# A hybrid attention and state-space layer on one core: the mixer's splits, loads, result tiles and squares in another order

## The chip, the cores and the metric

The kernel runs on one core of a Trainium2 chip. The metric is the device time of one execution in microseconds (us): the median of a few runs. In the text PE is the matrix engine (PEld its weight load), DVE the vector engine, ACT the scalar engine, POOL GpSimd, and SP the engine whose queue issues nearly all the DMAs.

## The reference, cut to what matters

One layer, 1024 positions of width 1024, all in float32. The part around the change is the state-space mixer (its scan runs in the kernel in chunks of 256 positions) and the projection of the attention's result beside it:

```python
X = (xh * dt[..., None])                    # 32 heads of 64, 8 groups, state 128
a_cum = jnp.cumsum(dt * A)                  # per head, inside a chunk
Lmat = jnp.exp(jnp.where(causal, a_cum[:, None] - a_cum[None, :], -inf))
CB = C @ B.T                                # per group
y_diag = (CB * Lmat) @ X
states = B.T @ (decay * X);  h = h * exp(a_cum[-1]) + states
y_off = exp(a_cum) * (C @ h_before)
y = y_diag + y_off + d_skip * xh
y_b = rmsnorm(y * silu(z), ssd_norm) @ w_o_ssd
mix = (sigmoid(g_a) * (attention @ w_o_attn) + sigmoid(g_b) * y_b) @ w_out
```

Then a residual sum and a SwiGLU block follow, which the change does not touch.

## The kernel before, in words

Every large product is made of three float32r matmuls: an operand is rounded to `hi` (on ACT) and the rest is kept as `lo` (on DVE or POOL), and hi·hi, hi·lo and lo·hi are added up. A "split" is this pair of instructions.

The **mixer stage** is a loop of 32 steps, n = 4·group + chunk (loop at the end of the excerpt), and one more for the last results. A step holds:

- `ssd_in(c, g)` for step n: SP loads `ld` (B, C and x: L1163, L1164) and `al` (the cumulative decays, broadcast to all partitions: L1169). ACT makes four M and four al rows with Relu (L1174, L1175) and two exponentials (L1176). PE makes `pcb` (C·B, L1179); DVE masks it (`cbm`) and multiplies it into al and M (L1184). PE transposes x (`px`) and B (`pbn`), and DVE and POOL make `X` and `Xd`.
- `ssd_out(c, g)` for step n−1: SP loads `zc` (the gate silu(z): L1215) and, but for a group's first chunk, `yt` (the decays of the state's share: L1218, two DMAs). PE makes `pyd` (the diagonal part, from al, M and X: L1224, L1225), `pst` (the chunk's state) and `pyo` (the part of the state so far: L1234). DVE multiplies and adds (L1236, L1237) and adds d_skip·x (L1241, two halves); POOL multiplies by the gate (L1243); SP stores the result to `d_y` (L1244). ACT squares the result for the norm (L1247), DVE adds the squares up (L1254), and the state is scaled on POOL and added to on DVE (L1258, L1260).

`zc` and `yt` share one tile, the **home** of a result: for n divisible by 3 it is the one tile `vt`, else one of the eight 1024-column tiles of the arena `R`, which also holds `ld` and `al`.

Beside each step PE does three or four slices of a **filler** (`beside`), six 128x512 matmuls each: first gate projections (pw, L244), then the projection of the attention's result (`poa`, L244). For the latter, sixteen tiles of the attention's result are loaded (`at_load`) and split (`at_split`, L1299, L1303), in four bursts of four, between tiles of the filler. `poa_run` loads a gate tile `ya` (L1321), and stores the product (L1325). Before the projection's last three tiles, `y_load` loads twelve half rows of `d_y` that the first groups have finished, and splits them (L1267, L1277, L1278), all in one burst.

After the last step the filler's rest runs alone, and then the **output projection** `pos` (L1647, seven products for a Strassen-like scheme in `SEQ`), whose inputs are sums and splits of `d_y` rows (`tasks`), and whose weights are split on ACT and POOL, later on ACT and DVE (L158, L159). Two norms (`ry`: p, L271, POOL's power L273, prn L279) and the merges with the attention's branch (`merge_first`, `gates_of`) are placed between its products.

PE's order is the order of the code (`in_order`). The order on ACT, DVE, POOL and SP is set by a scheduler from the code's order, its own timeline, the tiles' reuse and added "behind" dependencies (`add_manual_dep` with NoSync: an order on one engine, no wait). All four work their instructions off strictly in that order.

Of the kernel before, what the change touches and what calls it, by code (L numbers as in the profile page):

```python
# [69 lines left out]
def build(tc, a, dbg=None, stop=99, slots=None):  # L70
# [1084 lines left out]
    exps = [None]  # L1155

    def ssd_in(c, g, out):

# [4 lines left out]
        SP.dma_start(bc, d_bc[g].rearrange("j p l -> p j l")[:, :, cl])  # L1163
        SP.dma_start(xs, d_xs[2 * g:2 * g + 2].rearrange("j p l -> p j l")[:, :, cl])  # L1164
# [4 lines left out]
        SP.dma_start(al, d_ac[c, hs][None].to_broadcast([P, 4, QC]))  # L1169
# [37 lines left out]
    def ssd_out(c, g, z):  # L1207
# [4 lines left out]
        zy = (vp.tile([P, NT, P], F32, name="vt", bufs=1).rearrange("p (j x) n -> p j (x n)", j=4) if (4 * g + c) % 3 == 0  # L1212
              else R("zy", (P, 4, 256)))
        zc, yt = zy[:, 0:2], zy[:, 2:4]
        SP.dma_start(zc, d_z[2 * g:2 * g + 2].rearrange("j p l -> p j l")[:, :, cl])  # L1215
        if c:
            for e in range(2):
                SP.dma_start(yt[64 * e:64 * e + 64],  # L1218
                             d_ea[c, hs].rearrange("(j e) l -> e j l", e=2)[e:e + 1].to_broadcast([64, 2, QC]))
# [11 lines left out]
        if c:  # L1231
            pyo = bank("pyo")
            for j in range(2):
                T.matmul(pyo[:, 256 * j:256 * j + 256], st[:, 128 * j:128 * j + 128], CT, start=True, stop=True)  # L1234
            ytf = yt.rearrange("p j l -> p (j l)")
            V.tensor_tensor(ytf, ytf, pyo, op=OP.mult)  # L1236
            V.tensor_tensor(ytf, ytf, pyd, op=OP.add)  # L1237
        else:
            S.activation(yt.rearrange("p j l -> p (j l)"), pyd, AF.Copy)
        for j in range(2):  # L1240
            V.scalar_tensor_tensor(yt[:, j, :], xs[:, j], dsk[:, 2 * g + j:2 * g + j + 1], yt[:, j, :],  # L1241
                                   op0=OP.mult, op1=OP.add)
        G.tensor_tensor(yt, yt, zc, op=OP.mult)  # L1243
        SP.dma_start(d_y[2 * g:2 * g + 2].rearrange("j p l -> p j l")[:, :, cl], yt)  # L1244
        yield
        sq = Q("ysqt", (P, 2, 256))
# [8 lines left out]
        if c == 0:  # L1255
            S.activation(st, pst[:, 0:256], AF.Copy)
        elif c < NCH - 1:
            G.tensor_tensor(st.rearrange("p (h n) -> p h n", h=4), st.rearrange("p (h n) -> p h n", h=4),  # L1258
                            cdec[:, c, hs, None].to_broadcast([P, 4, 64]), op=OP.mult)
            V.tensor_tensor(st, st, pst[:, 0:256], op=OP.add)  # L1260
        yield
# [20 lines left out]
    def y_load(ks, places):  # L1282
        for k in ks:
            y_parts(1 + k // SK, k % SK, y_raw(k, 0), places(k), col("ssd_norm", k))

    def beside():
# [9 lines left out]
        def at_split(b, ks, where, raws):  # L1296
            for t, k in zip(raws, ks):
                hi, lo = where("ath", dt=F32R), where("atl", dt=F32R)
                i = S.activation(hi, t, AF.Copy).ins  # L1299
                for j in (ahead[0], *exps[0]):  # L1300
                    tc.add_manual_dep(i, j, mybir.DependencyInfo(
                        mybir.DependencyClass.NoSync, mybir.DependencyReason.DATA), reason="behind")
                (G if k % 2 else V).tensor_tensor(lo, t, f(hi), op=OP.subtract)  # L1303
                AT[k][0][b], AT[k][1][b] = hi, lo

# [13 lines left out]
        def poa_run(t, b, w):  # L1319
            ya = EV("ya")  # L1320
            SP.dma_start(ya, d_sga[t][:, half(b)])  # L1321
# [3 lines left out]
            SP.dma_start(d_ya[t][:, half(b)], ya)  # L1325
# [11 lines left out]
        at_split(*ld)  # L1337
        ld = at_load(0, range(AT_IN_Q, KT), H_)
        yield from gate_run(7, 0, w[1])
        at_split(*ld)  # L1340
        ld = at_load(1, range(4), H_)
        yield from gate_run(6, 1, w[0])
        at_split(*ld)
        ld = at_load(1, range(4, KT), H_)
        yield from gate_run(7, 1, w[1])
        w = two_tiles(a["w_o_attn"], (0, 1))
        yield from poa_run(0, 0, w[0])
        at_split(*ld)
# [815 lines left out]
```

## Time and profile before

| what | us |
|---|---|
| three runs: median (lowest, highest) | 2359.7 (2351.64, 2362.59) |
| the profiled execution's own time | 2361.0 |
| its span, first to last instruction | 2359.2 |
| PE busy in the span | 2308.6 (98%) |
| DVE, ACT, POOL busy | 1658.4, 1220.9, 988.0 |
| the mixer's steps: first and last pcb matmul | 1121.4 to 1420.9 |
| last scan result on PE (pyo) and first output projection | about 1438 and 1454 |

PE is busy nearly all the time, so time is to be had only where it waits or runs slowly. In a row of a timeline stand start, duration, engine, line, operation, output and inputs, and in brackets the idle time before the instruction and what ended it. A row of waits has: who waited, for whom, total us, times, longest.

### The profile page before, as it was taken

To read this page: it belongs to the slowest core of one execution; us is meant where nothing else is said; L and a number is where in the kernel's file an instruction comes from. 1 tells how busy PE (TensorE), PEld (TensorE's weight loads), DVE (VectorE), ACT (ScalarE), POOL (GpSimd) and SP (SyncE) were. 2 spreads that over 40 slices of the span, in tenths; PEclk is the share of its full clock that TensorE was granted. 3 is DMA by queue.
4 is the path that set the end of the run, shared out by engine and by line. 5 is a ranking of instruction groups with operands and counts; after the bars stand their busy time and mean duration, and the time that the engine had idled before them with its cause. 6 is when DMAs were issued, how large, how long until landed. Compare 5 with 4: busy or idle time off the path is not lost.

```text
span 2359.2 us, 35056 instructions
## 1 busy us (share of the span) xinstructions
PE 2308.6 (98%) x11736; PEld 1889.5 (80%) x11736; DVE 1658.4 (70%) x3185; ACT 1220.9 (52%) x2362; POOL 988.0 (42%) x787
## 2 busy tenths in 40 slices
PE   8999999999999999999999989999999999999997
PEld 5878888888888888887887777878788888888887
DVE  5467887499676767776678769865868776646675
ACT  4346666467645555556667565444555222235542
POOL 1435552522245656554445443000113445554556
PEclk8999999999999999999999999999999999999999
DMA  7137542622233433344679888864483444428664
GB/s 271 63 122 246 191 175 94 192 94 94 103 110 118 140 128 128 126 139 154 215 238 291 250 272 277 278 202 143 144 277 138 151 149 154 158 96 285 209 189 168
DMA packets 251716, 411.27 MB, mean 174 GB/s; under 512 B 25568, under 2 KB 93328, under 8 KB 251536
## 3 DMA queue, kind: packets, MB, share of 16 engines
q1 hardware_dynamic: 238288, 387.48, 49.2%
q10 hardware_dynamic: 13248, 21.56, 3.0%
q8 instruction: 92, 1.51, 0.3%
q14 instruction: 88, 0.72, 0.1%
HBM read 304.84 MB, written 107.24 MB: 175 GB/s over the span
## 4 chain that ended last, share of the span: by engine, by line
PE 74%; DVE 11%; DMA 7%; ACT 3%; issue 2%; POOL 1%; SPq 1%; DVEq 0%; ACTq 0%; POOLq 0%
PE p L1723 18%; PE pw L234 14%; PE pfo L1988 8%; PE pw L244 7%; PE plg L847 4%; PE pos L1647 3%; PE pot L1435 3%; PE prel L648 3%; PE pt L880 3%; PE po L896 3%; DVE junk L702 2%; PE puq L234 2%; DMA yl<-d_y 2%; PE poa L244 2%; DMA d_y<-zy 1%
## 5 line engine op out<-in xcount | busy, mean ns | idle before, releaser
L159 POOL TENSOR_TENSOR wlo<-wraw,whi 128x512 fp32r<-128x512 f32 x152 | 210.4, 1385 | 334.0 <-ACT whi L158 307.7
L1723 PE MATMUL p<-xh,wr 128*128 128x512 f32 x880 | 271.8, 389 | 0.0
L158 ACT ACTIVATE whi<-wraw 128x512 fp32r<-128x512 f32 x238 | 149.1, 627 | 214.0 <-issue 57.4
L1723 PEld LDWEIGHTS p<-xh,wr 128*128 128x128 f32 x880 | 165.2, 188 | 34.3
L1717 POOL TENSOR_TENSOR wr<-a,wr 128x512 fp32r<-128x512 f32 x82 | 115.2, 1413 | 134.0 <-ACT wr L1716 97.8
L1723 PE MATMUL p<-xl,wr 128*128 128x512 f32 x440 | 171.2, 389 | 0.0
L255 POOL TENSOR_TENSOR fwl<-fw,fwh 128x512 fp32r<-128x512 f32 (+1 forms) x78 | 106.7, 1377 | 104.0 <-ACT fwh L254 78.9
L1716 ACT ACTIVATE wr<-a 128x512 fp32r<-128x512 f32 x107 | 66.6, 629 | 127.5 <-PE p L1723 90.7
L859 ACT ACTIVATE lg<-lg,mx 128x256 f32<-128x256 f32 (+7 forms) x128 | 99.1, 774 | 58.3 <-DVE mx L856 50.8
L273 POOL TENSOR_TENSOR r<-v,nhalf 128x4 f32<-128x4 f32 (+1 forms) x17 | 20.0, 1178 | 260.7 <-DVE v L271 260.7
L654 DVE SCALAR_TENSOR_TENSOR acc<-rel,widx,acc 128x384 f32<-128x384 f32 (+2 forms) x90 | 102.9, 1168 | 15.8 <-ACT rel L649 15.6
L329 POOL TENSOR_TENSOR adaw<-adaw,cs 128x512 f32<-128x512 f32 x64 | 68.3, 1068 | 103.2 <-DMA adaw<-ada_w 93.1
L1723 PE MATMUL p<-h2h,wr 128*128 128x512 f32 x352 | 110.0, 390 | 0.0
L704 ACT ACTIVATE junk<-acc,cand__2216 128x1024 bf16<-128x1024 f32 (+2 forms) x96 | 86.2, 898 | 39.6 <-DVE cand__2216 L747 30.7
L649 ACT ACTIVATE rel<-prel 128x512 f32<-128x512 f32 (+3 forms) x160 | 76.9, 523 | 46.5 <-PE prel L648 43.3
L1723 PEld LDWEIGHTS p<-xl,wr 128*128 128x128 f32 x440 | 82.6, 188 | 17.1
L1647 PE MATMUL pos<-yh,wlo 128*128 128x512 f32 x224 | 87.9, 392 | 3.7 <-DVE wlo L159 2.3
L702 DVE TENSOR_SCALAR_CACHE_REDUCE junk<-acc,cand__2225 128x896 bf16<-128x896 f32 (+2 forms) x96 | 88.5, 922 | 1.5
L856 DVE CUSTOM_DVE_ANT_0 lg<-plg,nm 128x256 f32<-128x256 f32 (+1 forms) x128 | 51.5, 404 | 52.8 <-PE plg L847 52.1
L1647 PE MATMUL pos<-yh,whi 128*128 128x512 f32 x224 | 88.0, 393 | 0.5 <-ACT whi L158 0.4
L1717 POOL TENSOR_TENSOR wr<-s,wr 128x512 fp32r<-128x512 f32 x40 | 56.1, 1402 | 76.4 <-ACT wr L1716 69.2
L1647 PE MATMUL pos<-yw,whi 128*128 128x512 f32 x224 | 87.3, 390 | 0.0
(693 smaller groups left out, 7446.2 us busy)
## 6 DMA issues: line engine op xcount, KB each, us to landing
wraw<-w_in SPq DMA_DIRECT2D x129, 256.0 KB, 2.7
a<-w_ffn_in SPq DMA_DIRECT2D x122, 256.0 KB, 3.3
al<-d_a SPq DMA_DIRECT2D x88, 256.0 KB, 4.2
yl<-d_y SPq DMA_DIRECT2D x72, 256.0 KB, 4.6
adaw<-ada_w SPq DMA_DIRECT2D x64, 256.0 KB, 3.0
al<-d_ac SPq DMA_DIRECT2D x32, 512.0 KB, 5.2
d_a<-g SPq DMA_DIRECT2D x42, 256.0 KB, 2.4
ada<-ada_p SPq DMA_DIRECT2D x16, 512.0 KB, 7.6
```

Of the source, the lines that this page charges most:

```text
L158: self.hi = behind(S.activation(hi[:, :kt], raw[:, :kt], AF.Copy))
L159: self.lo = behind(self.eng[len(self.tiles) % len(self.eng)].tensor_tensor(lo[:, :kt], raw[:, :kt], f(hi[:, :kt]), op=OP.subtract))
L234: T.matmul(o, wt[:, k0 + i, :], xs[k][xi][b][:, sl], start=pi == 0 and i == 0 and wt is hi and xi == 0, stop=pi == len(pcs) - 1 and i == l ...
L244: T.matmul(o, wt[:, k0 + j, :], xs[k][xi][b], start=i == 0, stop=i == 23)
L255: (lo_eng or V).tensor_tensor(lo, src, f(hi), op=OP.subtract)
L654: V.scalar_tensor_tensor(acc[i][:, 0:n], rel[:, 0:n], ws, acc[i][:, 0:n], op0=OP.mult, op1=OP.add)
L702: V.tensor_scalar(jk, y, a_, 0.0, op0=op, op1=OP.add, accum_out=o)
L859: S.activation(lg[:, 0:n], lg[:, 0:n], AF.Exp, scale=-1.0, bias=m, accum_out=rr[:, 2 * t + hh:2 * t + hh + 1])
L1647: T.matmul(p, w[k // 4][wi][:, k % 4], YO[i][k][xi], start=start and k == 0 and n == 0, stop=k == SK - 1 and n == 2, skip_group_check=True)
L1717: parts_last[0] = parts_eng[0].tensor_tensor(w[:, 1], src, f(w[:, 0]), op=OP.subtract).ins.name
L1723: T.matmul(p, w[:, wi, i], X[x][i][xi], start=start and i == 0 and k == 0, stop=i == 3 and k == 2, skip_group_check=True)
L1988: T.matmul(p, w[wi][:, k - k0], xs[k][xi][:, sl], start=start and k == 0 and i == 0, stop=k == KH - 1 and i == 2, skip_group_check=True)
```

## The change

It does six things, all between about 1100 us and 1600 us of the span.

1. **Loads behind older stores.** The loads of `ld` and `al` of step n are put on SP behind the store of result n−4, those of `zc` and `yt` behind the store of result n−2, and the load of a gate tile `ya` behind the store of the product two before (`sp_behind`: order on SP alone).
2. **Three homes in turn.** Results of n mod 3 = 0 lie in `vt`, of 1 in the two tiles `adaw` of the weight pool (free in this stage), of 2 in a tile of `R`.
3. **d_skip·x first, in the PSUM bank.** DVE adds it to `pyd` in place (or, in a group's first chunk, from `pyd` into `yt`, which drops ACT's copy); the product with `pyo` and the sum follow.
4. **Squares a step later** (`squares`, called after the next step's first part), and the state's update ahead of them.
5. **Splits one per slice.** `at_split` and `y_load` return lists of jobs; `along` does one after each slice of the projection. The twelve `y` splits go four each along the last three projections, in the arena R in pairs, and stand behind the exponentials issued so far (`behind_exps`).
6. **Later norms and merges.** The two norms take their parts after products 3, 5, 7 and 10 of the output projection instead of after 0, 1, 2 and 3; the four first merges move back by one or two rounds of products.

```diff
+    def sp_behind(ins, stores, n):
+        if n in stores:
+            tc.add_manual_dep(ins.ins, stores[n], ... NoSync ...)
...
-        SP.dma_start(bc, d_bc[g].rearrange("j p l -> p j l")[:, :, cl])
-        SP.dma_start(xs, d_xs[2 * g:2 * g + 2].rearrange("j p l -> p j l")[:, :, cl])
+        sp_behind(SP.dma_start(bc, d_bc[g].rearrange("j p l -> p j l")[:, :, cl]), y_stores, n - 4)
+        sp_behind(SP.dma_start(xs, d_xs[2 * g:2 * g + 2].rearrange("j p l -> p j l")[:, :, cl]), y_stores, n - 4)
...
-        zy = (vp.tile([P, NT, P], F32, name="vt", bufs=1).rearrange("p (j x) n -> p j (x n)", j=4) if (4 * g + c) % 3 == 0
-              else R("zy", (P, 4, 256)))
+        if (4 * g + c) % 3 == 1:
+            zcf, ytf = (wp.tile([P, 4, P], F32, name="zy", tag="adaw", bufs=2).rearrange("p k m -> p (k m)") for _ in range(2))
+        else:
+            zy = vp.tile([P, NT, P], F32, name="vt", bufs=1).rearrange("p k m -> p (k m)") if (4 * g + c) % 3 == 0 else R("zy")
+            zcf, ytf = zy[:, 0:512], zy[:, 512:1024]
...
             V.tensor_tensor(ytf, ytf, pyo, op=OP.mult)
+        for j in range(2):
+            py = pyd[:, 256 * j:256 * j + 256]
+            V.scalar_tensor_tensor(py if c else yt[:, j], xs[:, j], dsk[:, 2 * g + j:2 * g + j + 1], py,
+                                   op0=OP.mult, op1=OP.add)
+        if c:
             V.tensor_tensor(ytf, ytf, pyd, op=OP.add)
-        else:
-            S.activation(yt.rearrange("p j l -> p (j l)"), pyd, AF.Copy)
-        for j in range(2):
-            V.scalar_tensor_tensor(yt[:, j, :], xs[:, j], dsk[:, 2 * g + j:2 * g + j + 1], yt[:, j, :],
-                                   op0=OP.mult, op1=OP.add)
         G.tensor_tensor(yt, yt, zc, op=OP.mult)
...
+        def along(run, jobs):
+            jobs = list(jobs)
+            for _ in run:
+                if jobs:
+                    jobs.pop(0)()
+                yield
+            for job in jobs:
+                job()
...
-            if bs == (0,):
-                y_load(range(12), y_place)
+                    n = 4 * (bs == (1,))
+                    yield from along(poa_run(t, b, w), [y_jobs.pop(0) for _ in range(n)])
...
                 next(g)
+                if i == 0 and done:
+                    squares(*done)
...
-            if n < 4:
-                next(norm[n // 2])
+            if n in (3, 5, 7, 10):
+                next(norm[n >= 7])
```

How the rows move on the engines' queues is shown at two places. The first is SP in the middle of the mixer; in the kernel before, these are the rows from the store of result 21 (`d_y<-vt`) to that of result 22:

```order
L1244 DMA d_y<-vt 128x2x256
L1163 DMA ld<-d_bc 128x2x256
L1164 DMA ld<-d_xs 128x2x256
L1215 DMA vt<-d_z 128x2x256
L1325 DMA d_ya<-ya 128x512
L1169 DMA al<-d_ac 128x1024
L1267 DMA yl<-d_y 128x512
L1244 DMA d_y<-zy 128x2x256
```

A load into `vt` stands four rows behind the store out of `vt`, and a load of a finished `d_y` row stands ahead of the next store. In the changed kernel the rows between the same two stores are:

```order
L1257 DMA d_y<-vt 128x2x256
L1228 DMA zy<-d_z 128x2x256
L1231 DMA zy<-d_ea 64x2x256 x2
L1172 DMA ld<-d_bc 128x2x256
L1173 DMA ld<-d_xs 128x2x256
L1178 DMA al<-d_ac 128x1024
L1373 DMA d_ya<-ya 128x512
L1369 DMA ya<-d_sga 128x512
L1257 DMA d_y<-zy 128x2x256
```

Behind a store now stand the loads of another home (that of result 23), then `ld` and `al` of step 25, and the `d_y` loads are gone from here.

The second place is ACT at the same steps. Before (`M`, `al`: Relu rows and exponentials of a step; `yh`: a split of a `d_y` row; `ysqt`: the squares; `whi`: a weight split):

```order
L1174 ACTIVATE M<-al,acum 128x128 x4
L1201 ACTIVATE bn<-pbn 128x256
L1175 ACTIVATE al<-al,acum 128x256 x4
L1176 ACTIVATE M<-M 128x512
L1277 ACTIVATE yh<-yl,vec 128x512
L1176 ACTIVATE al<-al 128x1024
L158 ACTIVATE whi<-wraw 128x512
L1247 ACTIVATE ysqt<-zy 128x512
```

And now:

```order
L1210 ACTIVATE bn<-pbn 128x256
L1183 ACTIVATE M<-al,acum 128x128 x4
L1184 ACTIVATE al<-al,acum 128x256 x4
L1185 ACTIVATE M<-M 128x512
L1185 ACTIVATE al<-al 128x1024
L158 ACTIVATE whi<-wraw 128x512
L1272 ACTIVATE ysqt<-zy 128x512
```

The `yh` between the two exponentials is gone; in the changed kernel all twelve stand behind the last exponentials of the mixer. The squares in such a row are now those of the result before the one that they squared there.

More of the change, by code (lines that the diff above doesn't have):

```diff
@@ L1155, in build @@
     exps = [None]
+    y_stores, ya_stores = {}, {}
+    def sp_behind(ins, stores, n):
+        if n in stores:
+            tc.add_manual_dep(ins.ins, stores[n], mybir.DependencyInfo(
+                mybir.DependencyClass.NoSync, mybir.DependencyReason.DATA), reason="behind")
     def ssd_in(c, g, out):
+        n = NCH * g + c
         hs = slice(4 * g, 4 * g + 4)
@@ L1168, in ssd_in @@
         al = R("al", (P, 4, QC))
[L1169 removed]
+        sp_behind(SP.dma_start(al, d_ac[c, hs][None].to_broadcast([P, 4, QC])), y_stores, n - 4)
         late_ = Q("M")
@@ L1280, in y_parts, with y_load, load, one @@
         return ins.ins
-    def y_load(ks, places):
-        for k in ks:
-            y_parts(1 + k // SK, k % SK, y_raw(k, 0), places(k), col("ssd_norm", k))
+    def y_load(ks, places, tie):
+        raws = {}
+        def load(k):
+            if k in ks and k not in raws:
+                t = R("yl", (P, 2, 512))
+                for j in range(2):
+                    raws[k + j] = t[:, j]
+                    SP.dma_start(t[:, j], d_y[k + j][:, half(0)])
+        def one(k):
+            load(k)
+            load(k + 2 - k % 2)
+            tie(y_parts(1 + k // SK, k % SK, raws[k], places(k), col("ssd_norm", k)))
+        return [lambda k=k: one(k) for k in ks]
     def beside():
@@ L1296, in at_split, with one, behind_exps @@
         def at_split(b, ks, where, raws):
-            for t, k in zip(raws, ks):
+            def one(t, k):
                 hi, lo = where("ath", dt=F32R), where("atl", dt=F32R)
[L1299 to L1302, printed above, removed]
+                behind_exps(S.activation(hi, t, AF.Copy).ins)
                 (G if k % 2 else V).tensor_tensor(lo, t, f(hi), op=OP.subtract)
                 AT[k][0][b], AT[k][1][b] = hi, lo
+            return [lambda t=t, k=k: one(t, k) for t, k in zip(raws, ks)]
+        def behind_exps(i):
+            for j in (ahead[0], *exps[0]):
+                tc.add_manual_dep(i, j, mybir.DependencyInfo(
+                    mybir.DependencyClass.NoSync, mybir.DependencyReason.DATA), reason="behind")
+        def along(run, jobs):
[3 more added lines that the diff above has]
+                    jobs.pop(0)()
+                yield
+            for job in jobs:
+                job()
         ahead = [None]
@@ L1320, in poa_run @@
             ya = EV("ya")
-            SP.dma_start(ya, d_sga[t][:, half(b)])
+            n = len(ya_stores)
+            sp_behind(SP.dma_start(ya, d_sga[t][:, half(b)]), ya_stores, n - 2)
             p = bank_d("poa")
@@ L1324, in poa_run @@
             i = V.scalar_tensor_tensor(ya, ya, 1.0, p, op0=OP.add, op1=OP.mult)
-            SP.dma_start(d_ya[t][:, half(b)], ya)
+            ya_stores[n] = SP.dma_start(d_ya[t][:, half(b)], ya).ins.name
             yield
@@ L1377, in build @@
                     k += 1
-            prev = s_ and (*s_, z)
+            done, prev = prev, s_ and (*s_, z)
+        squares(*done)
         for _ in filler:
```

55 lines of the change are left out of this document (29 added, 26 removed).

## Prediction

> **What bounds the kernel now.** I read the page first. PE is busy for 98% of the span, so the change can only give back what PE idles or runs slowly in the stretch that it touches. I therefore asked for the windows of that stretch next, 60 us each (span, then busy time of PE, PEld, DVE, ACT and POOL, then PE's clock, DMA share and GB/s):
>
> ```profile
> 1200.00:1260.00 60.00, 60.00 (x353) 48.32 (x352) 44.96 (x67) 39.66 (x90) 30.59 (x22) 1.00 0.82 264
> 1260.00:1320.00 60.00, 55.36 (x303) 44.03 (x305) 49.33 (x70) 41.46 (x92) 32.60 (x25) 0.97 0.86 274
> 1320.00:1380.00 60.00, 50.64 (x281) 39.83 (x278) 37.25 (x60) 35.04 (x81) 20.89 (x17) 0.91 0.84 254
> 1440.00:1500.00 60.00, 54.85 (x245) 42.83 (x244) 58.34 (x88) 33.30 (x58) 12.93 (x8) 1.00 0.93 309
> ```
>
> Up to 1260 PE never waits in the mixer. From 1260 to 1380 it idles 4.64 + 9.36 = 14.0 us and the clock drops; at the change to the output projection it idles 5.15 us. No engine is full in the mixer, so these are waits for something late, and the waits of PE from 1260 to 1500 say for what:
>
> ```profile
> PE pyd L1224 <- DVE al L1184: 11.1, 3, 7.1
> PE pcb L1179 <- DMA ld<-d_bc: 2.9, 2, 2.3
> PE pos L1647 <- POOL wlo L159: 1.4, 2, 0.8
> PE prn L279 <- POOL r L273: 1.4, 2, 0.9
> PE poa L244 <- POOL wlo L159: 1.0, 1, 1.0
> ```
>
> The first two rows are the mixer's 14.0 us; the other three are 3.8 of the 5.15 at the handoff. DVE is named for `pyd`, but DVE itself had waited. For the longest stall the timelines of ACT and of SP show for whom:
>
> ```profile
> 1354.60 0.62 ACT L1176 ACTIVATE M<-M 128x512 f32<-128x512 f32 x1
> 1362.92 0.72 ACT L1277 ACTIVATE yh<-yl,vec 128x512 fp32r<-128x512 f32 x1 [7.70 <-DMA yl<-d_y]
> 1363.55 1.04 ACT L1176 ACTIVATE al<-al 128x1024 f32<-128x1024 f32 x1
> ```
>
> ```profile
> 1348.61 0.63 SPq L1164 DMA_DIRECT2D ld<-d_xs  x1
> 1355.25 0.36 SPq L1215 DMA_DIRECT2D vt<-d_z  x1
> 1355.71 0.41 SPq L1325 DMA_DIRECT2D d_ya<-ya  x1
> 1356.22 0.37 SPq L1169 DMA_DIRECT2D al<-d_ac  x1
> 1359.22 0.32 SPq L1267 DMA_DIRECT2D yl<-d_y  x1
> ```
>
> An exponential that PE needed stood on ACT behind a split of a `d_y` row. That row's load was issued at 1359.22, because SP had stood still for 6.0 us before the load into `vt`, whose last result was still on its way out. So the chain is: store not landed, SP's queue stops, everything behind it is late, ACT's queue stops, PE stops. How often the two queues stop, from 1140 to 1440:
>
> ```profile
> SPq L1163 <- DMA d_y<-zy: 23.1, 7, 5.8
> SPq L1215 <- DMA d_y<-vt: 22.8, 9, 6.0
> SPq L1169 <- DMA d_y<-zy: 21.5, 10, 4.5
> ```
>
> ```profile
> ACT ysqt L1247 <- POOL zy L1243: 38.6, 17, 6.0
> ACT ysqt L1247 <- POOL vt L1243: 21.8, 7, 5.9
> ```
>
> SP loses 67.4 us to results that have not landed; ACT loses 60.4 us to squares that wait for POOL's product. Each is harmless until it meets an `al` or `ld` that is needed soon.
>
> **The change part by part.**
>
> *Loads behind stores, and three homes.* No DMA is added or removed, and the bytes stay the same. A load into a home now follows the store of the result that lay in it by one whole step: the home of result n was left by result n−3, and the load stands behind store n−2. A step is (1420.6 − 1121.4)/31 = 9.65 us by the row of `pcb`, and a result lands in 5.0 us, at most 7.9, by that of its store:
>
> ```profile
> L1179 PE MATMUL pcb<-ld x64: 377/377/463, 1121.4 to 1420.9; 128*128 128x256 f32 x64
> L1179 PEld LDWEIGHTS pcb<-ld x64: 186/188/192, 1121.4 to 1420.6; 128*128 128x128 f32 x64
> DMA to landing us min/median/max: 2.4/5.0/7.9
> ```
>
> So these 67.4 us of SP go, all but a rest. What SP waits for next is POOL's product, ahead of each store, and behind it are the loads for two and four steps later; they have 19 and 39 us for a landing of about 5. The second stall (2.3 us, `pcb` for `ld<-d_bc`) is an SP wait of this kind and goes.
>
> *Squares a step later.* ACT's 60.4 us of waiting go, since the result of two steps ago is there. What ACT waits for next is `pbn` from PE or `al`. The first stall (3.4 us) came from an `al` that was loaded late and an exponential that stood behind another step's rows; I count it as gone, with the most doubt.
>
> *Splits one per slice, `y` splits behind the exponentials.* The longest stall (7.1 us) is exactly the `yh` between two exponentials; in the new order all twelve stand behind the last exponentials. What they cost there: ACT 12 × 0.72 = 8.6 us by the row at 1362.92, among the last three tiles of the projection. PE needs the first of them only when `pos` begins, so the projection's matmuls cover them. Without that cover they would be worth up to 8.6 us.
>
> *d_skip·x in the bank.* Sixty-four half tiles, as before, but one operand and mostly the output lie in PSUM. The trace has the old form and, for whole tiles, the sum with `pyd`:
>
> ```profile
> L1241 DVE SCALAR_TENSOR_TENSOR zy<-ld,dsk,zy x42: 469/479/1559, 1145.8 to 1447.2; 128x256 f32<-128x256 f32 x42
> L1237 DVE TENSOR_TENSOR zy<-zy,pyd x16: 675/680/687, 1145.1 to 1443.5; 128x512 f32<-128x512 f32 x16
> ```
>
> Half of 0.68 to the whole of it is 0.34 to 0.68 us each, against 0.48: between −9 and +13 us of DVE time over the stage. I take 0.48, since the form has the same width. DVE has 10 to 23 us free in every 60 there, so I cost it at nothing.
>
> *The clock.* After the two long stalls PE runs slowly. A `pyd` to the next projection matmul takes 3.14 us at full speed (1337.78 to 1340.92), and 4.75 after the first stall. From `pyd` to the fourth projection matmul it takes 3.15 (1276.64 to 1279.79), and 5.94 after the third:
>
> ```profile
> 1276.64 0.66 PE L1224 MATMUL pyd<-al,X 128*64 128x256 f32 x4
> 1279.79 0.40 PE L244 MATMUL pw<-h5h,uh 128*128 128x512 f32 x1
> 1289.47 0.66 PE L1224 MATMUL pyd<-al,X 128*64 128x256 f32 x4 [3.36 <-DVE al L1184]
> 1294.22 0.58 PE L244 MATMUL poa<-ath,whi 128*128 128x512 f32 x1
> 1337.78 0.66 PE L1224 MATMUL pyd<-al,X 128*64 128x256 f32 x4
> 1340.92 0.59 PE L244 MATMUL poa<-ath,whi 128*128 128x512 f32 x1
> 1365.99 1.13 PE L1224 MATMUL pyd<-al,X 128*64 128x256 f32 x4 [7.08 <-DVE al L1184]
> 1371.93 0.39 PE L244 MATMUL poa<-ath,whi 128*128 128x512 f32 x1
> ```
>
> That is 1.6 + 2.8 = 4.4 us, which go with the stalls. [...]
>
> *Handoff.* The norms move two products apart, so `prn`'s 1.4 us go. The 2.4 us for `wlo` come from ACT, which splits weights late because it waits for `d_y` rows; fewer such rows stand ahead of them now, but the last store still does. Between 0 and 2.4 I take half, 1.2. Sum: 2.6.
>
> *New waits.* The trace cannot show them. The lower bound is 0, as up to 1260 in the first window; the upper one is a stall like today's longest with its slow clock, 7.1 + 2.8 = 9.9. I take one like the first, 3.4, because that was the stall of a queue that was only somewhat late.
>
> *Sum:* 14.0 + 4.4 + 2.6 − 3.4 = 17.6 us. The profiled execution took 2361.0 us (its span 2359.2), 1.3 above the median of the three runs: 2343.4 for it, and 2359.7 − 17.6 = **2342** for the median.
>
> **The rivals.**
>
> *All of it goes:* no new wait, and the handoff without a gap: 14.0 + 4.4 + 5.15 = 23.6 us, 2336. For it speaks the clean stretch before 1260; against it, that a gap of zero over 330 us has not been seen once the `atl` loads begin.
>
> *The DMA engines are the limit where the stalls begin.* Their busy share is highest just there, and again at the handoff:
>
> ```profile
> 1240.00:1260.00 20.00, 20.00 (x123) 15.90 (x122) 14.84 (x23) 14.58 (x33) 11.41 (x9) 1.00 0.99 328
> 1460.00:1480.00 20.00, 19.07 (x93) 15.70 (x94) 19.39 (x32) 14.40 (x26) 2.33 (x2) 1.00 0.96 344
> ```
>
> The bytes do not change, so the first stall with its slow clock and the two small ones (3.4 + 1.6 + 1.3 = 6.3) stay, and at the handoff only the norms' 1.4 go: 18.4 − 6.3 + 1.4 − 3.4 = 10.1 us, 2350. Against it: over 60 us the share is 0.86 at most up to 1380. [...]
>
> *Slower: the tie becomes a loop.* Store n−2 must be issued before the loads of result n, these must land before DVE and POOL can finish it, and only then is store n issued; all loads of later steps stand behind it. The loop has two steps, 19.3 us. In it lie the landing of the decays, two DVE instructions of 0.7 and POOL's product:
>
> ```profile
> DMA to landing us min/median/max: 3.1/5.3/8.6
> L1243 POOL TENSOR_TENSOR zy<-zy x21: 1264/1295/2253, 1146.8 to 1447.8; 128x512 f32<-128x512 f32 x21
> ```
>
> That is 5.3 + 1.4 + 1.3 = 8.0 us, and 12.3 with the longest of each. If SP also stops twice in it for other rows (6.0 and 4.5, its longest waits above), it is 22.8: 3.5 us too long, 15.5 times, 54 us, less the 21.0 that go: 2393. It decides from 19.3 us on, and gives a slower kernel from about 21.4. Against it: those SP waits are the ones that the homes remove.
>
> **How the numbers follow.** The forecast has 0.58, all of it 0.10, the DMA limit 0.23, the loop 0.09. A measurement of this kernel tells about 0.5% (11.8 us) from no change; the three runs lie 11 us apart. Faster by more than that, under 2347.9, are the first two cases: 0.68. Within it is the third: 0.23. Slower is the loop: 0.09. The range goes from the second case, less 1 us, 2335, to the third with the upper bound of the new waits (6.5 more), 2356, and 2 us for the spread: 2358.
>
> **What would show it right or wrong.** Right: in the new profile PE's waits for `al` and `ld` between 1260 and 1380 are under 4 us together, the granted clock stays at 1.00, SP's waits for `d_y` stores and ACT's for POOL's product (squares) are nearly gone, no `yh` stands between exponentials, and `prn` is not waited for. Wrong: a PE wait over 5 us at another place in the mixer, SP's waits moved to POOL's product with `al` late again, longer landings at an equal share, or `pos` waiting for `yh` or `yw`.

## The result and the profile after

The changed kernel takes 2333.17 us (median of four runs, 2332.83 to 2334.56) where the kernel before took 2359.03 beside it (2351.64 to 2362.59). The ratio is 0.9896, with a 95% interval of 0.9871 to 0.992: 25.9 us less, where 17.6 were forecast, and 1.8 us under the low end of the range. The profiled execution took 2334.56 us, its span is 2332.5. The sign and the place were right, the size was not.

The same windows of the changed kernel (span, then busy time of PE, PEld, DVE, ACT and POOL, PE's clock, DMA share, GB/s):

```profile
1260.00:1320.00 60.00, 60.00 (x354) 48.24 (x353) 54.32 (x74) 49.13 (x111) 38.39 (x28) 1.00 0.92 297
1320.00:1380.00 60.00, 60.00 (x344) 48.67 (x343) 43.91 (x75) 37.51 (x83) 23.89 (x21) 1.00 0.90 276
1380.00:1440.00 60.00, 60.00 (x307) 48.66 (x307) 53.53 (x78) 36.80 (x69) 27.59 (x20) 1.00 0.94 313
1440.00:1500.00 60.00, 59.17 (x271) 48.38 (x270) 51.58 (x85) 33.27 (x57) 10.08 (x2) 1.00 0.83 279
```

In this profile PE no longer waits in the mixer at all, its clock stays at 1.00, and the DMA engines are busier than before (0.92 and 0.90 for 0.86 and 0.84) without holding PE up. What is left of PE's waits up to the end of the output projection's `pos` stands in one row:

```profile
PE pos L1698 <- DVE wlo L159: 2.1, 4, 0.8
```

The mixer's matmuls are the same ones in both kernels, so I measure two lengths: the **mixer**, from the first `pcb` to the last `pyo` matmul, and the **handoff**, from there to the last `pos`. Their windows, mixer and handoff, in the kernel before:

```profile
1121.40:1438.50 317.10, 303.10 (x1711) 242.98 (x1711) 230.55 (x343) 206.06 (x460) 146.16 (x110) 0.98 0.79 251
1438.50:1662.40 223.90, 216.87 (x962) 176.30 (x960) 162.43 (x251) 101.79 (x176) 15.72 (x10) 1.00 0.67 221
```

and in the changed one:

```profile
1116.40:1414.20 297.80, 297.80 (x1713) 240.28 (x1712) 224.76 (x345) 203.22 (x449) 139.10 (x110) 1.00 0.85 267
1414.20:1631.70 217.50, 215.34 (x962) 176.79 (x961) 157.95 (x248) 104.22 (x178) 20.72 (x10) 1.00 0.68 226
```

The mixer is 19.3 us shorter: 14.0 of idling and 5.3 of slower running. The handoff is 6.4 us shorter: 4.9 of idling (7.03 to 2.16) and 1.5 of running. Together they are 25.7. Ahead of the mixer and behind the handoff the code is the same and the two profiles differ by -5.0 and +4.0, which is scatter: over all profiles below, the first `pcb` lies anywhere from 1115.3 to 1121.4, and the part behind the last `pos` takes 696.7 to 701.4. A second profile of the changed kernel (a_again below) gives 18.1 + 4.8 = 22.9, so the two shares are known to a few us, not to tenths.

SP's and ACT's waits in the mixer after the change (1140 to 1440):

```profile
SPq L1257 <- POOL zy L1256: 36.8, 16, 4.7
SPq L1257 <- POOL vt L1256: 24.5, 9, 5.3
...
SPq L1178 <- DMA d_y<-zy: 3.7, 4, 1.6
```

```profile
ACT ysqt L1272 <- POOL zy L1256: 22.7, 13, 3.8
...
ACT ysqt L1272 <- POOL vt L1256: 10.3, 8, 2.6
```

SP still stands still for as long as before (61.3 us against 67.4), but now ahead of a store, for POOL's product. The loads behind it come in time, but by little. The prediction gave them 19 and 39 us to spare. In fact a result is stored some two steps after its step's first matmul, so the `al` of step 19, which stands behind the store of result 15 (1271.98), is issued 9.0 us ahead of its own step's first matmul (1287.17), and ACT waits for it:

```profile
1278.15 0.46 SPq L1178 DMA_DIRECT2D al<-d_ac  x1
1285.04 1.28 ACT L1183 ACTIVATE M<-al,acum 128x128 f32<-128x128 f32 x4 [2.46 <-DMA al<-d_ac]
```

ACT waits so in eight steps, 9.1 us in all (in six steps and 5.7 us in the second profile), and none of it reaches PE. From step 4 on each `al` is now issued 7.5 us or more ahead of its step's first matmul; in the kernel before, the `al` of step 25 (the row at 1356.22 in the prediction) was issued 0.2 us after it. ACT's squares still wait for POOL for 33.0 us of the 60.4.

### The profile page after: what moved, and what is told of

Same layout as the page of the kernel before. It is cut to its first block, busy times and chain, and to the rows that moved or that the text cites. A ratio compares the mean times of both kernels' runs of the same rounds, so it can differ in the third digit from the quotient of the medians.

```text
span 2332.5 us, 35045 instructions
## 1 busy us (share of the span) xinstructions
PE 2298.1 (99%) x11736; PEld 1886.0 (81%) x11736; DVE 1646.2 (71%) x3185; ACT 1220.1 (52%) x2354; POOL 985.3 (42%) x787
## 5 line engine op out<-in xcount | busy, mean ns | idle before, releaser
L273 POOL TENSOR_TENSOR r<-v,nhalf 128x4 f32<-128x4 f32 (+1 forms) x17 | 25.5, 1499 | 255.4 <-DVE v L271 255.4
```

## The experiments

All runs in one table. "Idle" is PE's idle time in the stretch, times are medians of four runs or more, and the lengths are those of one profile each; the kernel before ran beside each set at 2360.5 to 2361.4. Names that begin with u_ undo a part of the changed kernel, names with o_ put parts into the kernel before, names with x_ add something to the changed kernel. The scheduler makes its order anew for each, so an edit can move rows at other places too.

| kernel | mixer | idle | handoff | idle | time |
|---|---|---|---|---|---|
| before | 317.1 | 14.0 | 223.9 | 7.0 | 2359.0 |
| changed | 297.8 | 0.0 | 217.5 | 2.2 | 2333.2 |
| a_again: changed once more | 299.0 | 1.1 | 219.1 | 3.2 | 2335.8 |
| u_ties: no order on SP | 324.1 | 16.4 | 236.5 | 14.1 | 2381.7 |
| u_homes: two kinds of homes | 300.0 | 2.1 | 222.0 | 4.4 | 2342.2 |
| u_squares: squares at once | 299.0 | 0.7 | 221.4 | 5.3 | 2339.2 |
| u_early: y splits earlier | 301.3 | 2.8 | 223.3 | 7.0 | 2343.5 |
| u_bursts: at splits in bursts | 298.9 | 1.0 | 218.6 | 3.3 | 2336.8 |
| u_ysplits: y splits in one burst | 299.0 | 1.1 | 224.5 | 6.7 | 2341.9 |
| u_handoff: norms as before | 299.1 | 1.1 | 217.9 | 2.1 | 2335.7 |
| u_dskip: d_skip as before | 300.5 | 2.5 | 221.6 | 4.3 | 2337.2 |
| u_tight: zc, yt behind n-1 | 317.9 | 14.4 | 226.3 | 7.1 | 2362.6 |
| u_loose: zc, yt behind n-3 | 298.3 | 0.1 | 224.1 | 5.7 | 2341.3 |
| o_ties: order on SP | 310.3 | 8.1 | 220.4 | 4.2 | 2350.4 |
| o_loads: and homes | 307.6 | 8.3 | 223.2 | 6.1 | 2349.0 |
| o_loads_splits: and splits | 305.3 | 5.7 | 222.9 | 5.9 | 2348.4 |
| o_lsd: and d_skip | 299.0 | 0.7 | 220.9 | 4.3 | 2337.0 |
| o_handoff: norms alone | 320.1 | 16.3 | 225.3 | 7.3 | 2360.0 |
| x_pool: every second wlo on POOL, 4 products | 299.1 | 1.1 | 220.1 | 3.6 | 2338.4 |
| x_pool8: the same, 8 products | 297.8 | 0.0 | 222.6 | 5.3 | 2339.4 |

The changed kernel against itself (a_again) gives the spread: 1.2 us of mixer, 1.6 of handoff, 2.6 of time. The 1.1 us of idling that several variants show is one wait, absent in the first profile of the changed kernel and there in its second:

```profile
PE pbn L1208 <- DVE vt L1249: 1.1, 1, 1.1
```

So a mixer from 297.8 to 299.1 and a handoff from 217.5 to 219.1 are as in the changed kernel. The kernel before scatters more: o_handoff leaves its mixer as it was, and that took 320.1 us, 3.0 more.

> The changed kernel once more, unaltered, for the spread of the two lengths by which all these runs are compared. Expected: the mixer 297.8 to 299.2 us (three variants whose order in the mixer is hardly or not altered took 298.9 to 299.1), the handoff 217 to 218.5, the time 2333 to 2335.

The handoff and the time came out 0.6 and 0.8 us above what was expected.

**The order on SP.** u_ties undoes it alone:

```diff
-        if n in stores:
+        if False and n in stores:
```

> The changed kernel without the order on SP behind older stores; the three homes, the squares a step later and the spread splits stay. Measure: the mixer from the first pcb to the last pyo matmul (317.1 us before, 297.8 changed) and PE's idle time in it (14.0 and 0). Theory A (SP's stops before results that have not landed are the root: the queue stops, al or ld is late, PE stops): the rows of loads move back ahead of stores that have not landed; SP's waits for d_y stores, 3.7 us at L1178 in the changed kernel, come back to 20 us or more, and the mixer takes 300 to 308 us, the time 2336 to 2344. Theory B (ACT's row is the root: a y split between two exponentials, squares that wait): SP's waits come back too, but the mixer stays within 1 us of 297.8, the time within 2 us of 2333. Theory C (the homes alone take SP's waits away): these waits stay under 8 us and the time at 2333.

It takes 1.0099 of the time before (1.0078 to 1.012): the other parts without the order are a loss of 20 us. The mechanism is theory A's, the size more than twice what A gave (324.1 us, for 300 to 308), and the handoff is 17 to 19 us longer as well, which no theory had. SP's waits in its mixer, and one of ACT's (1120 to 1440):

```profile
SPq L1228 <- DMA d_y<-vt: 39.9, 10, 6.9
SPq L1178 <- DMA d_y<-zy: 29.8, 7, 6.6
SPq L1231 <- DMA d_y<-zy: 22.0, 7, 5.2
```

```profile
ACT M L1183 <- DMA al<-d_ac: 75.8, 19, 6.6
```

SP's rows show how at one place (start, duration, line):

```profile
1285.53 0.38 SPq L1257 DMA_DIRECT2D d_y<-vt  x1
1286.05 0.38 SPq L1363 DMA_DIRECT2D d_gb<-g  x1
1286.56 0.42 SPq L157 DMA_DIRECT2D wraw<-w_o_attn  x1
1290.97 0.37 SPq L1228 DMA_DIRECT2D vt<-d_z  x1
1291.44 1.77 SPq L1325 DMA_DIRECT2D atl<-d_att  x2
1293.30 0.38 SPq L1178 DMA_DIRECT2D al<-d_ac  x1
```

Three rows behind the store out of `vt` stands a load into it. SP stops from 1286.98 until the store has landed, and `al`, which goes into another tile, comes 2.3 us behind that load. The three rows of SP's waits make 91.7 us, against 67.4 for the three rows of the kernel before; the homes alone do not remove them. C falls, and B.

**Its distance.** u_loose and u_tight change only behind which store `zc` and `yt` stand:

```diff
-..., y_stores, n - 2)
+..., y_stores, n - 3)    in u_loose, n - 1 in u_tight
```

> The changed kernel with the loads of zc and yt one step looser: behind the store of result n-3 instead of n-2, which is the store out of the very home that they load into. One step tighter cost 20 us of the mixer, no order at all 26. Theory A: the load now may stand right behind the store out of its home, SP stops for the landing as before (d_y stores, 20 us or more at L1228), and PE idles 2 us or more in the mixer: 301 to 312, time 2336 to 2348. Rival (the scheduler places these loads later by itself, the order of ld and al is what matters): SP's waits at L1228 under 8 us, mixer 298 to 300, time 2333 to 2336.

> The changed kernel with the loads of zc and yt one step tighter: behind the store of result n-1 instead of n-2. It leaves the computation as it is. It tests the slower case of the prediction: the loop from load to result to store to load must then fit into one step of 9.3 us instead of two, and takes 8.0 us with typical and 12.3 with the longest durations. Loop theory: it binds in part of the steps, ACT and SP wait for results, PE idles 15 us or more in the mixer, which takes 315 us or more, the time 2350 or more. Rival (nothing on PE needs a result before the output projection, and the banks between PE and DVE cover a late one): POOL and SP wait more, PE under 4 us, mixer under 302, time under 2340.

One step looser, SP's waits for stores are back at 40.8 us:

```profile
SPq L1178 <- DMA d_y<-zy: 14.2, 8, 2.8
SPq L1228 <- DMA d_y<-vt: 14.1, 7, 4.2
SPq L1231 <- DMA d_y<-zy: 12.5, 6, 3.5
```

PE feels none of it in the mixer (0.1 us idle), but the handoff is 5 to 6.6 us longer: the mixer (298.3) is as the rival had it, the time (2341.3) as theory A had it, and by which way SP's waits reach the handoff was not shown. One step tighter, the loop binds as the slower rival of the prediction said it would beyond its limit: DVE waits for decays that are still on their way, 6.7 us in the row below against 0.0 and 0.5 in the changed kernel's two profiles, PE waits for loads that stand behind a store on SP, and the mixer is 19 to 20 us longer.

```profile
DVE zy L1249 <- DMA zy<-d_ea: 6.7, 7, 2.8
```

```profile
PE pcb L1188 <- DMA ld<-d_bc: 10.5, 7, 2.4
```

**Homes, squares and early y splits undone.**

```diff
-        if (4 * g + c) % 3 == 1:
-            zcf, ytf = (wp.tile(... tag="adaw", bufs=2) ... for _ in range(2))
-        else:
-            zy = vp.tile(...) if (4 * g + c) % 3 == 0 else R("zy")
+        zy = vp.tile(...) if (4 * g + c) % 3 == 0 else R("zy")
```

> The changed kernel with the homes as before (vt for n divisible by 3, else a tile of the arena R); order on SP, squares and splits stay changed. Theory A: tiles of R are again left by results that have not landed when ld or al is loaded into them, so SP waits for d_y stores 15 to 45 us in the mixer and PE stalls in it by 2 to 8 us: mixer 300 to 306, time 2335 to 2342. Theory B (ACT's row is the root): the waits on SP come back, PE's stall does not: mixer within 1 us of 297.8, time within 2 us of 2333. Theory C, turned round (the order on SP alone suffices): waits under 8 us and 2333.

With the order on SP but the old homes, SP waits 23.4 us for stores, PE idles 2.1 us in the mixer and 1 to 2 more in the handoff: A at its low end for the mixer and at its high end for the time, since the handoff had not been in the sum. PE's 2.1 us are the wait of `pbn` again that a_again has with 1.1, so for the mixer this lies hardly beyond the spread.

```profile
SPq L1172 <- DMA d_y<-zy: 23.4, 15, 4.0
```

```diff
-        z["yt"] = yt
+        z["yt"] = yt; squares(c, g, z)
...
-                if i == 0 and done:
-                    squares(*done)
```

> The changed kernel with the squares back in the step that makes the result; all else stays changed. ACT's waits of ysqt for POOL's product were 60.4 us before and are 33.0 in the changed kernel. Theory A: they come back to 50 to 65 us, but as al and ld arrive early ACT makes it up, and PE's stall in the mixer stays under 2 us: mixer 298 to 300, time 2333 to 2336. Theory B (ACT's row is the root): the first stall of before (3.4 us with its slow clock of 1.6) comes back: mixer 301 to 304, time 2337 to 2340.

ACT's waits for POOL's product come back to 56.6 us, and PE idles 0.7 us in the mixer: A there, but the handoff is 2 to 4 us longer, so that the time (2339.2) lies where B had put it.

```diff
-        y_jobs = y_load(range(12), y_place, behind_exps)
+        y_jobs = y_load(range(12), y_place, lambda i: None)
...
-                    n = 4 * (bs == (1,))
+                    n = 4 * (bs == (0,))
```

> The changed kernel with the twelve y splits along the three slices before the last three and without the order behind the exponentials: four of them then stand ahead of the exponentials of step 30 and one between the last two. Loads behind stores, homes and squares stay changed. Theory A (SP is the root): the rows of d_y have landed when ACT gets to them, or are late by under 2 us, so a split between exponentials costs ACT its 0.72 us and PE at most 1 us: mixer 298 to 300, time 2333 to 2335. Theory B (the split between exponentials is the root, wherever SP stands): ACT waits for a d_y row by 3 to 8 us again, PE stalls for al by 3 to 7 us with the slow clock behind it: mixer 302 to 308, time 2338 to 2344.

The mixer (301.3) lies between the two, the time (2343.5) in B's range: ACT waits for rows of `d_y` by 7.6 us in four places (at most 3.0), PE by 1.0 for `al`. A y split between exponentials costs something even when loads are in order, but far less than the 7.1 us of the kernel before.

**Parts put in one after another.** o_ties and o_loads take the diff's `sp_behind`, then also its homes, into the kernel before.

> The kernel before with one part of the change: the loads of ld, al, zc, yt and ya ordered on SP behind older stores; homes, squares, splits, d_skip and handoff as before. Theory A, as the undone parts left it (the order on SP carries the mixer's gain: without it the changed kernel's mixer took 324.1 us, with all but the homes 300.0): PE's idle time in the mixer falls from 14.0 to under 4 us, the mixer from 317.1 to 300 to 304, the time from 2360 to 2343 to 2350. Rival (the parts only work together, each undone part cost something because the others were in): SP's waits for d_y stores fall, but a y split or a square keeps al late on ACT; the mixer takes 307 us or more, the time 2350 or more.

> The kernel before with two parts: the order on SP and the three homes. Theory A: SP's waits for d_y stores are under 10 us in the mixer as in the changed kernel, the mixer takes 298 to 302 us, the time 2341 to 2348, with the handoff as long as before (about 224 us from the last pyo to the last pos, 217.5 in the changed kernel). Rival (squares and splits are needed too): PE idles by 4 us or more in the mixer, which takes 304 or more, the time 2348 or more.

Both rivals held. The stalls at 1316, 1346 and 1366 of before are gone. The first two were waits for `ld` and so SP's. At the third the scheduler has also moved the y splits: in o_ties none stands on ACT ahead of 1408, so how much of those 7.1 us the earlier load alone would have saved is not shown. The homes add little behind the order (8.1 and 8.3 us idle, 2350.4 and 2349.0 us). And in o_loads, where SP hardly waits for a store any more, 8.3 us for `al` are left (PE's rows, then the row in ACT's timeline that holds the last):

```profile
1285.24 1.13 PE L1238 MATMUL pyd<-al,X 128*64 128x256 f32 x4 [3.40 <-DVE al L1193]
...
1419.75 0.66 PE L1238 MATMUL pyd<-al,X 128*64 128x256 f32 x4 [3.52 <-DVE al L1193]
```

```profile
1406.16 1.39 ACT L1290 ACTIVATE yh<-yl,vec 128x512 fp32r<-128x512 f32 x2 [5.83 <-DMA yl<-d_y]
```

The first stall of before stands there unaltered, so it was not a late load. In the kernel before, its rows are these:

```profile
1278.29 1.74 POOL L1243 TENSOR_TENSOR vt<-vt 128x512 f32<-128x512 f32 x1
1280.06 0.63 ACT L1247 ACTIVATE ysqt<-vt 128x512 f32<-128x512 f32 x1 [1.19 <-DMA al<-d_ac]
```

The profile names a DMA for the wait of the square, but POOL's product ended at 1280.03, so the square waited for that. From there ACT worked without a gap until 1288.15, when the exponential that PE needed was done; DVE, which multiplies it, was busy for 18.65 of the 19.0 us up to 1290.1. So both engines were full for those 8 us, though over 60 us they are not. The last stall is new: a y split stands ahead of a later step's exponentials and waits there for its row.

> The kernel before with three parts: the order on SP, the three homes and the splits one per slice (the twelve y splits behind the exponentials); squares, d_skip and handoff as before. With the first two parts alone PE still idled 8.3 us for al: 3.40 at 1285, 1.07 at 1315, 3.52 at 1420. Theory F (what is left is ACT's row: bursts of splits, and a y split that waited 5.83 us for its row ahead of the exponentials): all three go, the mixer takes 298 to 300 us instead of 307.6, the time 2338 to 2343. Rival (squares that wait for POOL's product, still in their old place, hold ACT): the stall at 1285 stays, PE idles 3 us or more for al, the mixer takes 302 or more, the time 2343 or more.

With the splits (the diff's `along`, `at_split` and `y_load`) the new stall goes, but PE still waits for `al` 2.50 us at 1288 and 1.98 at 1311, as the rival had it. ACT's timeline ahead of the second:

```profile
1302.91 0.63 ACT L1260 ACTIVATE ysqt<-zy 128x512 f32<-128x512 f32 x1 [8.14 <-POOL zy L1256]
1303.44 1.27 ACT L1183 ACTIVATE M<-al,acum 128x128 f32<-128x128 f32 x4
1304.62 1.70 ACT L1184 ACTIVATE al<-al,acum 128x256 f32<-128x256 f32 x4
1306.21 0.62 ACT L1185 ACTIVATE M<-M 128x512 f32<-128x512 f32 x1
1306.73 1.05 ACT L1185 ACTIVATE al<-al 128x1024 f32<-128x1024 f32 x1
```

A square waits for POOL's product, and the rows that PE needs stand behind the square. Two parts of the change bear on that: the squares' move, and d_skip, which shortens the way to the product. o_lsd adds d_skip to the last kernel, u_dskip takes it out of the changed one:

```diff
-        for j in range(2):
-            py = pyd[:, 256 * j:256 * j + 256]
-            V.scalar_tensor_tensor(py if c else yt[:, j], xs[:, j], dsk..., py, ...)
         if c:
             V.tensor_tensor(ytf, ytf, pyd, op=OP.add)
+        else:
+            S.activation(ytf, pyd, AF.Copy)
+        for j in range(2):
+            V.scalar_tensor_tensor(yt[:, j, :], xs[:, j], dsk..., yt[:, j, :], ...)
```

> The kernel before with four parts: the order on SP, the three homes, the splits one per slice and d_skip in the bank; squares and handoff as before. Theories H and I: the mixer takes 298 to 300 us instead of 305.3 without d_skip's part, PE idles under 1.5 us in it, the time is 2340 to 2343. Rival (something else in the changed kernel, such as the order of squares and state): 303 to 306, 2345 to 2349.

> The changed kernel with d_skip times x as before: two vector instructions behind the sum, both operands in SBUF, and ACT's copy of the bank in a group's first chunk. It asks for the part of the mixer's gain that the order on SP, the homes and the splits leave: with these three alone the mixer took 305.3 us, in the changed kernel without the squares' move 299.0, in the changed kernel 297.8. Theory H (d_skip in the bank brings POOL's product forward, so that squares hold ACT less): the mixer takes 302 to 306 us, the time 2337 to 2343. Rival I (with the squares a step later a late product holds nobody, so either of the two suffices): 298 to 300, 2333 to 2337. The prediction costed this part at nothing, between 9 us of DVE less and 13 more.

d_skip in the bank ends the stalls without the squares' move (5.7 us of idling to 0.7, mixer 305.3 to 299.0); without it but with the move, 1.5 us of mixer come back (300.5 against 299.0). H falls, and rival I holds within a microsecond: either nearly suffices. The edit does two things, it shortens the way to POOL's product and drops ACT's copy of the bank, and these were not taken apart. The time of o_lsd, 2337.0, is 3 us below the range that was forecast.

```diff
-        jobs = at_split(*ld)
+        for job in at_split(*ld): job()
...
-        yield from along(gate_run(7, 0, w[1]), jobs)
+        yield from gate_run(7, 0, w[1])
```

> The changed kernel with the splits of the attention's result in four bursts of four as before (the y splits stay changed). Theory F: the first stall of before comes back, 2 to 4 us of PE for al near 1280, mixer 301 to 304, time 2336 to 2340. Rival (the squares' place took it away): PE's idle time in the mixer stays under 1.2 us, mixer 298 to 299, time 2333 to 2335.

The rival held, at a time (2336.8) 1 us above that of a_again: the bursts of four do no harm once the loads are in time and the squares are out of the way.

**The handoff.** First the norms, alone in the kernel before and undone in the changed one:

```diff
-            if n in (3, 5, 7, 10):
-                next(norm[n >= 7])
+            if n < 4:
+                next(norm[n // 2])
```

> The kernel before with one part: the later norms and merges of the output projection. From the last pyo to the last pos it takes 223.9 us before and 217.5 changed, with PE idling 7.0 and 2.2 us. Theory D (the norms' share): PE no longer waits for POOL's power (1.4 us) nor for what that delays, the stretch takes 221 to 223 us, the time falls by 1 to 3 us, to 2357 to 2359. Theory E (the norms' place holds up DVE and so all weight splits): the stretch takes 217 to 219 and the time falls by 5 to 7. The mixer stays at 317 by both.

> The changed kernel with norms and merges at their old places. Theory D: the wait for POOL's power comes back (1.4 us and the refill of PE), the stretch from the last pyo to the last pos takes 219 to 221 us instead of 217.5, the time 2335 to 2337. Theory E: 223 or more, 2339 or more. The mixer stays at 298 by both.

Both theories fall by the handoff. Alone, the later norms end the wait of `prn`, but `pos` waits for DVE's `wlo` 4.6 us instead of 2.3, the handoff takes 225.3 us, and the time is 0.9998 of that before (0.9985 to 1.0011). Undone in the changed kernel, `prn` does not wait either, and the handoff stays at 217.9. So no gain by the norms' place is seen; one of a microsecond or two these times could not tell.

```diff
-        y_jobs = y_load(range(12), y_place, behind_exps)
...
+            if bs == (0,):
+                for k in range(12): y_parts(1 + k // SK, k % SK, y_raw(k, 0), ...)
```

> The changed kernel with the twelve y splits in one burst ahead of the last three projection tiles, not ordered behind the exponentials, each row in its own tile; all else stays changed. In its order all twelve stand behind the last exponentials all the same, so the mixer is expected at 298 to 299 us by every theory. They tell apart what shortened the handoff (last pyo to last pos: 223.9 before, 217.5 changed, 217.9 with the norms at their old places, so not the norms). Theory G (twelve y splits ahead of the weights' splits on ACT make wlo late): 220 to 224 us and a time of 2336 to 2340. Rival (the handoff follows from whatever the mixer leaves late): 217 to 219 and 2333 to 2335.

G held, at 0.5 us and 2 us above its ranges: the handoff takes 224.5 us, 5 to 7 more, with PE waiting 6.6 us for weights. DVE is busy for 98% or more of the 40 us that begin 20 us behind the last `pyo` in every kernel but u_ties (87%); in the changed one it is full from 1428 to 1473:

```profile
1428.00:1448.00 20.00, 20.00 (x90) 16.55 (x89) 20.00 (x32) 15.19 (x28) 0.80 (x1) 1.00 1.00 363
1448.00:1473.50 25.50, 24.67 (x113) 19.76 (x112) 25.50 (x43) 15.28 (x26) 2.67 (x1) 1.00 0.93 314
```

If its backlog sets the handoff, taking some weights' low parts to POOL, which is idle, should shorten it:

```diff
-        W.eng[:] = [V]
+        W.eng[:] = [V, G]
         for n, x in enumerate(SEQ):
+            if n == 4: W.eng[:] = [V]
```

> The changed kernel with every second low part of a weight (wlo) on POOL instead of DVE in the first four products of the output projection; POOL has 10 us of work in the 60 there, DVE has none free from 1428 to 1473. Theory J (the handoff is set by DVE's backlog, so whatever the mixer leaves late for DVE lengthens it): PE's waits for DVE's wlo, 2.1 to 3.2 us in the changed kernel's two profiles, fall under 1.5, the handoff takes 215.5 to 217.5 instead of 217.5 to 219.1, the time 2331 to 2334. Rival (POOL's 1.46 us for one, and the two holding each other up, cost as much): waits for POOL's wlo take their place, handoff 218 to 222, time 2334 to 2338.

> The same over the first eight products. Theory J: as with four, or 0.5 us better: handoff 215 to 217.5, time 2331 to 2334, no wait of PE for wlo over 0.5 us up to 1560. Rival: as with four, and worse by the further waits: handoff 219 to 224, time 2335 to 2340.

The rival held, with the first only just beyond the spread: handoffs of 220.1 and 222.6 us, times of 2338.39 and 2339.44 us. POOL's `wlo` took 1.71 us each in x_pool, and DVE's own rows beside it grew; one of them in the changed kernel, then in x_pool (busy us, mean ns):

```profile
L1617 DVE SCALAR_TENSOR_TENSOR yl<-yl,vec 128x512 f32<-128x512 f32 x8 | 5.9, 739 | 0.4 <-DMA yl<-d_y 0.4
```

```profile
L1617 DVE SCALAR_TENSOR_TENSOR yl<-yl,vec 128x512 f32<-128x512 f32 x8 | 9.6, 1196 | 0.4 <-DMA yl<-d_y 0.4
```

That is 3.7 us more for DVE (2.7 against the second profile of the changed kernel, 866 ns), where POOL had taken four low parts of 0.68. DVE was not relieved, so this does not test whether its backlog is the cause; that stays open. Shown is that the handoff lengthens when any part but the norms' and the bursts' is undone, also where the mixer does not. It does not simply add up: the order on SP alone already brings it from 223.9 to 220.4, and with the homes it is 223.2 again.

## Why the prediction was wrong in size

The sum was 14.0 + 4.4 + 2.6 - 3.4 = 17.6; measured by the same terms, it is 14.0 + 5.3 + 6.4 - 0 = 25.7 (14.0 + 5.2 + 4.8 - 1.1 = 22.9 with the second profile). Two steps failed.

- **New waits** (3.4 taken, 0 measured, 1.1 in the second profile). The step reasoned that a queue that is only somewhat late would stall PE once more. With a part of the change that is just what happens: o_ties and o_loads have a new stall of 3.4 and 3.5 us, a y split ahead of the exponentials. The order of the y splits behind the exponentials, another part of the same diff, takes it away (o_loads_splits), and the step priced the two parts without each other.
- **Handoff** (2.6 taken, 6.4 measured, 4.8 by the second profile). Its 1.4 us for the norms were wrong: undoing their move costs nothing that is seen. Its 1.2 were half of the two waits for POOL's `wlo`; in fact every wait there but DVE's 2.1 us went, and 1.5 us of slower running too. I had looked for the gain in the handoff's own edits, and it comes with parts that act in the mixer and at its end: undone one by one, the spread of the y splits costs the handoff 5 to 7 us, the distance of the order on SP 5 to 6.6, homes, squares and d_skip 2 to 4.5 each, which overlap. By which way they reach the handoff stays open; a backlog on DVE is a candidate that was not shown.

Point by point for the rest:

- *The chain* from a store over SP to PE was right for the stalls at 1316 and 1346, which the order on SP alone removes. At 1366 it removes the stall too, with the y splits moved. There I also left out a link: directly ahead of the load at 1359.22 SP waited once more, 2.5 us for the store of a product of the projection (`d_ya<-ya`).
- *The first stall* I put to a late load, with the most doubt, and that was wrong: o_loads left it at 3.40 us, o_loads_splits had 2.50 there, and it went with d_skip (o_lsd), where the square that stands ahead of `al` on ACT waits 0.94 us instead of 3.26 and ACT has a copy less. That its 3.4 us are in the 14.0 all the same is luck.
- *The time to spare* for the loads, 19 and 39 us, was counted in steps from the result's number. Results are stored late, and `al` came 7.5 to 15 us ahead of its step's first matmul: enough for PE, not for ACT.
- *SP's waits* went from stores that had not landed to POOL's product, 61.3 us, and cost PE nothing, as said.
- *ACT's 60.4 us of waiting* were to go; 33.0 stayed, and PE did not feel them.
- *d_skip*, costed at nothing, was a mistake that the sum does not show. The old form took (21.8 + 13.8)/62 = 0.57 us in the mean, by the rows of 62 of the 64, not the 0.48 of the median that I used; the new one (23.3 + 4.3 + 2.6)/64 = 0.47. That is 64 times 0.10, 6.5 us of DVE over the stage, inside the bounds given, and it lies on the way to POOL's product. Put in behind the first three parts it is worth 6.3 us of mixer. The squares' move hides it.
- *The clock.* PE's busy time in the mixer fell by 5.3 us, for 4.4; over the whole mixer the granted clock was 0.98 in the kernel before and 1.00 in the changed one, and what of the 5.3 is the clock was not taken apart.
- *The rivals.* "All of it goes" (2336) came nearest, and the range ended 1 us below it. It too was short, by 0.9 for the clock and 1.3 at the handoff, where it counted only the idle time of one 60 us window (5.15). "The DMA engines are the limit" falls: their share is 0.90 to 0.94 where PE never waits. "The tie becomes a loop" needs one step instead of two, and then costs 19 to 20 us of mixer.

## What to carry to other kernels

On a queue that runs strictly in order, price a wait by what stands behind it and not by its length: 61 us of SP's waits ahead of stores cost PE nothing, waits ahead of loads that were needed soon stopped it. Put a load behind an event that is surely over (here a store two results back; three back was too loose, one too tight), read from a trace how much time is then left for it, and test such an order by taking it out of the finished change: alone it took 6.8 us off the mixer, taken out it put 26 on. Where a change feeds an engine that is full right behind it, charge or credit that stretch too: a fifth to a quarter of this gain was there.

## What the runs showed of the hardware

- **DVE and POOL took longer side by side.** In the kernel before, the two halves of d_skip·x take 1.97 and 1.90 us beside POOL's work and 0.88 where POOL waits. POOL's rows, and DVE's, there:

```profile
1275.62 2.70 POOL L1303 TENSOR_TENSOR atl<-atl,ath 128x512 fp32r<-128x512 f32 x2 [0.87 <-ACT ath L1299]
...
1279.98 1.49 POOL L159 TENSOR_TENSOR wlo<-wraw,whi 128x512 fp32r<-128x512 f32 x1
...
1298.22 1.29 POOL L1243 TENSOR_TENSOR zy<-zy 128x512 f32<-128x512 f32 x1 [2.05 <-DVE zy L1241]
```

```profile
1275.22 1.97 DVE L1241 SCALAR_TENSOR_TENSOR vt<-ld,dsk,vt 128x256 f32<-128x256 f32 x2
1279.86 1.90 DVE L1241 SCALAR_TENSOR_TENSOR zy<-ld,dsk,zy 128x256 f32<-128x256 f32 x2
1297.26 0.88 DVE L1241 SCALAR_TENSOR_TENSOR zy<-ld,dsk,zy 128x256 f32<-128x256 f32 x2
```

  Of the 64 halves, the 48 that no row of POOL overlaps took 0.47 to 0.49 us, the 16 that one overlaps 0.47 to 1.58. With one operand in PSUM none of 48 is stretched (the longest takes 491 ns, for 1559 to 1575 before), though rows of POOL overlap 25 of them, and POOL's product fell from 1.53 and 1.49 us to 1.32 and 1.29 in the mean:

```profile
L1252 DVE SCALAR_TENSOR_TENSOR pyd<-ld,dsk,pyd x48: 475/489/491, 1137.2 to 1414.0; 128x256 f32<-128x256 f32 x48
```
- **DMA at 363 GB/s.** From 1428 to 1448 the core moved 363 GB/s in the changed kernel with the DMA share at 1.00, and PE was busy for 20.00 of 20 us.
- **Two stalls of one length, two clocks.** In o_loads PE idled 3.40 us up to 1285.24 and 3.52 us up to 1419.75. The first four matmuls behind the one took 1.13 us, those behind the other 0.66; the granted clock was 0.97 over the 60 us from 1260 and 1.00 over the 60 us from 1380. In this run the length of a stall alone did not tell whether the clock drops.
- **Landings.** With the DMA share in the mixer up from 0.79 to 0.85, the stores of the results landed sooner, in 3.4 us in the median instead of 5.0. Why was not tried. The row of the stores in the changed kernel:

```profile
DMA to landing us min/median/max: 2.1/3.4/7.4
```
